# A decoder layer on one core: GpSimd's elementwise work in the mixer handed to VectorE, ScalarE and transposed rows

## The chip, the core and the metric

The kernel runs on one core of a Trainium2 chip. Its time is the device time of one execution in microseconds (us). The core has a matrix engine (TensorE, PE in the profile), a vector engine (VectorE, DVE), a scalar engine (ScalarE, ACT), a general engine (GpSimd, POOL) and a fifth one that here only starts transfers (SyncE, SP). Each engine takes its own queue in order and meets the others at semaphores.

## What is computed

One step of a decoder layer for two groups, a prompt of 1024 rows and 8 samples of one row, all of width 1024 in float32. First a mixer, then a gated feed-forward network; each is modulated by a condition and followed by a gated residual with a layer norm. The mixer has one input projection of 2816 columns, then two kinds of heads side by side, and one output projection:

```python
q, k, v, rq, rk, rv, rg = project_in(h, w_in)
...
rq = rope(rq.reshape(B, L, RET_HEADS, RET_DK), pos, RET_DK, RET_THETA)
rk = rope(rk.reshape(B, L, RET_HEADS, RET_DK), pos, RET_DK, RET_THETA) * (RET_DK ** -0.5)
...
def retention_output(o, g, gn_w):
    mu = jnp.mean(o, -1, keepdims=True)
    var = jnp.mean(jnp.square(o - mu), -1, keepdims=True)
    n = ((o - mu) * lax.rsqrt(var + GN_EPS)).reshape(o.shape[0], o.shape[1], RET_WIDTH)
    n = n * gn_w.astype(jnp.float32)
    return (jax.nn.silu(g.astype(jnp.float32)) * n).astype(g.dtype)
```

Attention (8 heads of 64, window 128) isn't touched by the change. Retention (4 heads of 128) rotates queries and keys, works over the prompt in 8 chunks of 128 rows with a state that decays by a constant of each head, and for each sample applies one step to a state of 4 heads x 128 x 128 that is read, updated and written back. Its output is normed per head, multiplied by the norm weight gn_w (one value for each of 512 columns) and by the gate silu(rg).

## The kernel before

Every large product is made of three matmuls (mm3, L215 to L217): each factor is split into a high part and a residual (wh and wl for weights, hT or mh and ml for rows), so each weight block needs a cast on ScalarE (wh, L269) and a subtraction on VectorE (wl, L281) before PE can use it. These blocks stream in by SyncE's queue (raw).

The prompt goes through the mixer in two halves of 512 rows. In order of time: a start with the modulation and the first projection (to about 66 us), the input projection of half 0 (to about 212), that of half 1 with attention and retention of half 0 and the samples beside it (to about 432), the output projection with the retention chunks of half 1 (pout, to about 565), then the feed-forward network. A small planner (Merge) takes pieces of work from several Python generators, by costs that these yield, and so fixes the order in the program; a tile scheduler then sets each engine's queue from it. So an edit that adds an instruction also shifts others in the queues.

The functions that matter:

- ropefull rotates 512 columns: a product with the cosines into its output (GpSimd), two half products with the sines into a temporary, and the sum (VectorE). It is called twice for each chunk (rr) and twice for the samples (rrs).
- ret_prep does both rotations of a chunk, scales its values by the decay (vg from zkv, GpSimd) and calls gate_prep, which makes the gate in the other half of vg and multiplies it by half of the norm weight, gnwh (GpSimd).
- ret_O and gnorm make the normed and gated rows sm of a chunk. ret_M transposes them by head on PE (bank rmt) and splits them into pages mh and ml, which the output projection takes. These pages belong to a half and not to a chunk.
- samp_ret loads the states st in four pages, scales them by gam (GpSimd), adds the new outer products (VectorE, 32 pieces) and writes them back. Its queries and keys are transposed in the bank srt from rrs.
- out_samp sums the four row groups of the samples' output projection (poutz) by samp_sum in a temporary from tmp512, a ring of three buffers shared with ropefull (rtmp) and with the evictions of pout (otmp, out_evac L1112 and L1113).

GpSimd also does the power in the norms (grs, lrs) and starts some transfers.

Of the kernel before, what the change touches and what calls it, by code (L numbers as in the profile page):

```python
# [13 lines left out]
ALU = mybir.AluOpType  # L14
# [163 lines left out]
def emit(ctx, tc, I, O):  # L178
# [133 lines left out]
    sinkb = small("sinkb", [128, 8])  # L312
    nsink = small("nsink", [128, 8])
    sink64 = small("sink64", [128, 2])
    gnwh = small("gnwh", [128, 512])
    ffs = hTs
    identr = small("identr", [128, 128], 1, F32R)

# [391 lines left out]
    def ropefull(out, x, cos, sin, rows):  # L710
        xv = x.rearrange("p (h s d) -> p h s d", h=4, s=2)
        ov = out.rearrange("p (h s d) -> p h s d", h=4, s=2)
        tmp = tmp512("rtmp")
        tv = tmp[0:rows].rearrange("p (h s d) -> p h s d", h=4, s=2)
        sb = sin.unsqueeze(1).to_broadcast([rows, 4, 64])
        G.tensor_tensor(out=ov, in0=xv, in1=cos.unsqueeze(1).unsqueeze(1).to_broadcast([rows, 4, 2, 64]), op=ALU.mult)
        V.scalar_tensor_tensor(out=tv[:, :, 0], in0=xv[:, :, 1], scalar=-1.0, in1=sb, op0=ALU.mult, op1=ALU.mult)
        V.tensor_tensor(out=tv[:, :, 1], in0=xv[:, :, 0], in1=sb, op=ALU.mult)
        V.tensor_tensor(out=out, in0=out, in1=tmp[0:rows], op=ALU.add)
# [7 lines left out]
    def gate_prep(dst, rg, rows):  # L727
        A.activation(out=dst, in_=rg, func=AF.Tanh, scale=0.5)
        yield 0, 1000
        V.scalar_tensor_tensor(out=dst, in0=dst, scalar=1.0, in1=rg, op0=ALU.add, op1=ALU.mult)  # L730
        G.tensor_tensor(out=dst, in0=dst, in1=gnwh[0:rows], op=ALU.mult)

    def gnorm(o, n_out, gate, rows, scaled, pe, dve):
        st = small("gst", [128, 4, 6], 2)
# [21 lines left out]
    def ret_prep(c):  # L756
        rr = page(f"rr{c}")
        vg = page(f"vg{c}")
        tab = tab_box[0]
        cos, sin = tab[:, c * 64:(c + 1) * 64], tab[:, 512 + c * 64:576 + c * 64]  # L760
        ropefull(rr[:, 0:512], zqg[c][:, 0:512], cos, sin, 128)
        yield 0, 1000, 1300
        ropefull(rr[:, 512:1024], zkv[c][:, 0:512], cos, sin, 128)
        G.tensor_tensor(out=h4(vg[:, 0:512]), in0=h4(zkv[c][:, 512:1024]), in1=bc4(C("vsc"), 128), op=ALU.mult)
        yield 0, 1000, 1300
        yield from gate_prep(vg[:, 512:1024], zqg[c][:, 512:1024], 128)
        R[c] = {"rr": rr, "vg": vg}
        zkv.pop(c)
        zqg.pop(c)
# [52 lines left out]
    def ret_M(c):  # L822
        sm = R.pop(c)["sm"]
        b = bank("rmt")
        for h in range(4):
            PE.transpose(b[:, h * 128:(h + 1) * 128], sm[:, 512 + h * 128:640 + h * 128], ident)
        half, tl = c // 4, c % 4
        for j in range(2):
            mh, ml = mix_pages(half, 2 + j)
            src = b[:, j * 256:(j + 1) * 256].rearrange("p (a c) -> p a c", a=2)  # L830
            oh = mh[:, 0:1024].rearrange("p (a c) -> p a c", a=2)[:, :, tl * 128:(tl + 1) * 128]
            ol = ml[:, 0:1024].rearrange("p (a c) -> p a c", a=2)[:, :, tl * 128:(tl + 1) * 128]
            A.copy(out=oh, in_=src)
            V.tensor_sub(out=ol, in0=src, in1=f(oh))

    def ret_chunk(c):
        yield "need", ("in", c // 4, "rg")
# [107 lines left out]
    def samp_ret():  # L945
        yield "need", ("zs", "rv")
        zkvs, zqgs = zs["r"][32:40], zs["r"][0:8]
        vd = drp.tile([8, 512], F32, name="vd")
        G.dma_start(out=vd, in_=zkvs[:, 512:1024])
        yield "need", ("zs", "rq")  # L950
        state_pg = []
        for i in range(4):
            t = page(f"st{i}")
            SP.dma_start(out=t[:, 0:1024].rearrange("p (a e) -> p a e", a=8),
                         in_=I["state"][8 * i:8 * i + 8].rearrange("a d e -> d a e"))
            state_pg.append(t)
        rr = page("rrs")
        ropefull(rr[0:8, 0:512], zqgs[:, 0:512], C("src")[0:8], C("srs")[0:8], 8)
        ropefull(rr[0:8, 512:1024], zkvs[:, 0:512], C("src")[32:40], C("srs")[32:40], 8)
        vb = []  # L960
        for i in range(4):
            t = page(f"vb{i}")
            SP.dma_start(out=t[:, 0:1024], in_=vd[2 * i:2 * i + 2, :].rearrange("(o b) e -> o (b e)", o=1)
                         .to_broadcast([128, 1024]))
            vb.append(t)
        yield 0, 4000, 3000
        b = bank("srt")
        for i in range(8):
            PE.transpose(b[:, i * 8:(i + 1) * 8], rr[0:8, i * 128:(i + 1) * 128], ident[0:8, 0:8])
        qs = small("qss", [128, 32])  # L970
        ks = small("kss", [128, 32])
        V.tensor_copy(out=qs.rearrange("p (b h) -> p h b", b=8), in_=b[:, 0:32].rearrange("p (h b) -> p h b", h=4))
        V.tensor_scalar(ks.rearrange("p (b h) -> p h b", b=8), b[:, 32:64].rearrange("p (h b) -> p h b", h=4),
                        128.0 ** -0.5, None, op0=ALU.mult)
        yield 200, 800
        qm = page("qm")[:, 0:256]
        G.memset(qm, 0.0)
        qm4 = qm.rearrange("p (b h r) -> p b h r", b=8, h=4)
        for s in range(8):
            V.tensor_copy(out=qm4[:, s, :, s], in_=qs[:, 4 * s:4 * s + 4])  # L980
        bo = bank("sro")
        for i in range(4):
            st = state_pg[i]
            G.tensor_tensor(out=st[:, 0:1024].rearrange("p (b h e) -> p b h e", b=2, h=4),
                            in0=st[:, 0:1024].rearrange("p (b h e) -> p b h e", b=2, h=4),
                            in1=C("gam").unsqueeze(1).unsqueeze(3).to_broadcast([128, 2, 4, 128]), op=ALU.mult)
            for j in range(8):
                bh = 8 * i + j
                sl = slice(j * 128, (j + 1) * 128)
                V.scalar_tensor_tensor(out=st[:, sl], in0=vb[i][:, sl], scalar=ks[:, bh:bh + 1], in1=st[:, sl],  # L990
                                       op0=ALU.mult, op1=ALU.add)
            yield 0, 4500, 2200
            for j in range(8):
                bh, h = 8 * i + j, j % 4
                PE.matmul(bo[32 * h:32 * h + 8, 0:128], lhsT=qm[:, bh * 8:bh * 8 + 8], rhs=st[:, j * 128:(j + 1) * 128],
                          start=i == 0 and j < 4, stop=i == 3 and j >= 4)
            SP.dma_start(out=O["nrs"][8 * i:8 * i + 8].rearrange("a d e -> d a e"),
                        in_=st[:, 0:1024].rearrange("p (a e) -> p a e", a=8))
            yield 430, 0
        yield "need", ("zs", "rg")  # L1000
        gt = page("gts")
        yield from gate_prep(gt[0:8, 0:512], zqgs[:, 512:1024], 8)
        yield 0, 1500
        so = tmp512("so")
        for h in range(4):
            A.copy(out=so[0:8, h * 128:(h + 1) * 128], in_=bo[32 * h:32 * h + 8, 0:128])
        yield from gnorm(so[0:8, :], gt[0:8, 512:1024], gt[0:8, 0:512], 8, False, 0, 1300)
        yield 0, 1200
        b = bank("smt")
        for h in range(4):  # L1010
            PE.transpose(b[:, h * 8:(h + 1) * 8], gt[0:8, 512 + h * 128:640 + h * 128], ident[0:8, 0:8])
        V.tensor_copy(out=mixTs[:, 4:8, 0:8], in_=b[:, 0:32].rearrange("p (h b) -> p h b", h=4))
        done.add("mixs_r")
        yield 100, 0

# [98 lines left out]

    def out_samp(cg, psz):
        cs = slice(cg * 512, (cg + 1) * 512)
        tmp = tmp512("otmp")
        samp_sum(tmp[0:8], psz, 512)
        V.tensor_tensor(out=tmp[0:8], in0=tmp[0:8], in1=gates[1, "s"][0:8, cs], op=ALU.mult)
        x = xrs[0]  # L1120
        V.scalar_tensor_tensor(out=x[0:8, cs], in0=x[0:8, cs], scalar=ALPHA, in1=tmp[0:8], op0=ALU.mult, op1=ALU.add)
# [648 lines left out]
    def misc_loads():  # L1770
        tc.keep_in_program_order(SP.dma_start(out=sinkb, in_=I["sinks"].to_broadcast([128, 8])))
        tc.keep_in_program_order(SP.dma_start(out=sink64[0:64, 0:1], in_=I["sinks64"]))
        tc.keep_in_program_order(SP.dma_start(out=gnwh, in_=I["gn_w"].to_broadcast([128, 512])))
        G.tensor_scalar(nsink, sinkb, -1.0, None, op0=ALU.mult)
        G.tensor_scalar(sink64[0:64, 1:2], sink64[0:64, 0:1], -1.0, None, op0=ALU.mult)
        G.tensor_scalar(gnwh, gnwh, 0.5, None, op0=ALU.mult)
        t = page("tab")
        SP.dma_start(out=t[:, 0:1024], in_=I["tab"])
        tab_box.append(t)
# [84 lines left out]
```

## Time and profile before

| | |
|---|---|
| runs | 1281.33, 1281.74, 1282.64 us; median 1281.74 |
| profiled execution | 1281.65 us, its span 1279.8 us |
| mean granted clock of TensorE | 0.975 |
| busy: TensorE, VectorE, ScalarE, GpSimd | 1218.8, 883.8, 449.3, 152.6 us |
| GpSimd's product with the cosines, L716 | 16 of 128x512, 1368 and 1443 ns each; 2 of 8x512, 1164 ns |
| GpSimd's product with the norm weight, L731 | 8 of 128x512, 1724 ns each; 1 of 8x512, 2336 ns |
| GpSimd's scaling of the values, L764 | 8 of 128x512, 1112 ns each |
| GpSimd's scaling of the states, L984 | 4 of 128x1024, 2074 ns each |

A row of a list of waits reads: engine, tile and line that waited, then the engine, tile and line that released it, then the sum in us, the number of waits and the longest. A row of a timeline reads: start, duration, engine, line, operation, tiles and shapes, and in brackets the engine's idle time just before with its releaser. A row of windows reads: stretch and its length, then for each engine its busy time and in brackets its instructions, then the granted clock (PEclk, 1.00 is full), the share of the transfer engines and GB/s. A row of groups ends in busy us, mean ns of one, and the idle time ahead.

### The profile page before, as it was taken

How to read it: one execution, taken by the hardware profiler on the slowest of the kernel's cores; microseconds unless marked ns; L12 is line 12 of the kernel's file. 1: busy time of each engine (PE TensorE's matmuls, PEld its weight loads, DVE VectorE, ACT ScalarE, POOL GpSimd, SP SyncE). 2: the span in 40 equal slices, each digit the busy share in tenths (PEclk: the TensorE clock that was granted, in tenths of full speed). 3: DMA queues.
4: the chain of work that ended last, by engine and by line, in shares of the span. 5: the costliest groups of instructions: out<-in, count | busy, mean ns of one | idle time of the engine just before them, and what ended most of it. 6: DMA issues, size and time to landing. Idle time of an engine off the chain costs nothing.

```text
span 1279.8 us, 20189 instructions
## 1 busy us (share of the span) xinstructions
PE 1218.8 (95%) x7922; PEld 1026.1 (80%) x7922; DVE 883.8 (69%) x1712; ACT 449.3 (35%) x812; POOL 152.6 (12%) x170
## 2 busy tenths in 40 slices
PE   8999979999999989797999999999999999999996
PEld 5877756778777758576999999999999987888885
DVE  2456665787655587696777766767676759849697
ACT  2335523344553223536323222322233234534420
POOL 0000031321002231110101110111101110000011
PEclk8999989899999989989999999999999999999999
DMA  9732477152225332502334443543354399846631
GB/s 284 238 112 67 134 243 266 50 172 80 67 66 205 126 103 71 198 33 87 119 119 167 145 160 108 178 150 135 121 169 157 124 338 398 276 154 212 201 126 66
DMA packets 144136, 199.07 MB, mean 156 GB/s; under 512 B 8140, under 2 KB 85172, under 8 KB 144025
## 3 DMA queue, kind: packets, MB, share of 16 engines
q1 hardware_dynamic: 133512, 161.37, 39.3%
q0 software_dynamic: 10528, 36.42, 7.5%
q8 instruction: 62, 1.02, 0.3%
q14 instruction: 34, 0.27, 0.1%
HBM read 155.02 MB, written 43.77 MB: 155 GB/s over the span
## 4 chain that ended last, share of the span: by engine, by line
PE 36%; issue 34%; DVE 8%; POOL 5%; DMA 2%; ACT 1%; POOLq 0%; DVEq 0%; SPq 0%; ACTq 0%
PE dn L216 4%; PE dn L217 4%; PE dn L215 4%; PE pin L215 4%; PE pin L216 3%; PE pin L217 3%; PE pout L216 2%; POOL fd L1485 1%; PE pout L217 1%; PE pout L215 1%; POOL fs L1489 1%; POOL ws L1518 1%; PE adab L874 1%; DVE z L1595 1%; DMA z<-yd 1%
## 5 line engine op out<-in xcount | busy, mean ns | idle before, releaser
L215 PE MATMUL pin<-wh,hT 128*128 128x512 f32 (+1 forms) x320 | 129.6, 409 | 0.1
L216 PE MATMUL pin<-wl,hT 128*128 128x512 f32 (+1 forms) x320 | 125.6, 393 | 3.8 <-DVE wl L281 3.8
L217 PE MATMUL pin<-wh,hT 128*128 128x512 f32 (+1 forms) x320 | 125.0, 392 | 0.4 <-DVE hT L340 0.4
L215 PE MATMUL up<-hb,wa_h 128*128 128x256 f32 (+1 forms) x352 | 100.2, 285 | 2.0 <-ACT hb L1300 1.5
L216 PE MATMUL up<-hb,wa_h 128*128 128x256 f32 (+1 forms) x352 | 100.0, 284 | 0.7 <-DVE hb L1301 0.7
L217 PE MATMUL up<-hb,wa_l 128*128 128x256 f32 (+1 forms) x352 | 99.6, 283 | 0.4 <-DVE wa_l L1347 0.4
L215 PEld LDWEIGHTS pin<-wh,hT 128*128 128x128 f32 x320 | 61.0, 191 | 26.5 <-issue 13.5
L281 DVE TENSOR_TENSOR wl<-raw,wh 128x1024 fp32r<-128x1024 f32 (+1 forms) x62 | 74.0, 1195 | 7.1 <-PE ptp L657 3.5
L217 PEld LDWEIGHTS pin<-wh,hT 128*128 128x128 f32 x320 | 61.6, 193 | 16.1 <-issue 2.2
L216 PEld LDWEIGHTS pin<-wl,hT 128*128 128x128 f32 x320 | 62.0, 194 | 14.5 <-DVE wl L281 4.3
L1452 ACT ACTIVATE sg<-sg 128x256 f32<-128x256 f32 (+1 forms) x66 | 27.7, 420 | 120.9 <-DVE sg L1451 120.9
L215 PEld LDWEIGHTS up<-hb,wa_h 128*128 128x128 f32 x352 | 66.9, 190 | 2.9 <-ACT hb L1300 1.9
L216 PEld LDWEIGHTS up<-hb,wa_h 128*128 128x128 f32 x352 | 67.0, 190 | 1.3 <-DVE hb L1301 1.3
L217 PEld LDWEIGHTS up<-hb,wa_l 128*128 128x128 f32 x352 | 66.6, 189 | 0.7 <-DVE wa_l L1347 0.7
L269 ACT CAST wh<-raw 128x1024 fp32r<-128x1024 f32 (+1 forms) x62 | 62.8, 1022 | 11.4 <-DMA raw<-in_w_in 6.6
L216 PE MATMUL pout<-wl,mh 128*128 128x512 f32 x128 | 53.0, 415 | 13.6 <-DVE wl L281 13.6
L1457 DVE TENSOR_TENSOR uc<-up,tp 128x256 f32<-128x256 f32 x66 | 28.2, 427 | 39.0 <-PE up L217 38.9
L1451 DVE TENSOR_TENSOR sg<-up,tp 128x256 f32<-128x256 f32 (+1 forms) x66 | 27.9, 423 | 38.2 <-PE up L217 38.2
L1485 POOL DMA_DIRECT2D fd<-sg x33 | 19.8, 599 | 280.2 <-DVE sg L1458 280.2
L1471 ACT COPY hTs<-sg 128x8 f32<-128x8 f32 x22 | 4.3, 198 | 138.8 <-DVE sg L1458 138.8
L215 PE MATMUL pout<-wh,mh 128*128 128x512 f32 x128 | 52.8, 418 | 0.0
L217 PE MATMUL pout<-wh,ml 128*128 128x512 f32 x128 | 52.2, 409 | 0.0
(502 smaller groups left out, 3695.9 us busy)
## 6 DMA issues: line engine op xcount, KB each, us to landing
wr<-in_w_up SPq DMA_DIRECT2D x44, 512.0 KB, 5.4
raw<-in_w_in SPq DMA_DIRECT2D x38, 512.0 KB, 4.0
adr<-in_w_ada_ffn SPq DMA_DIRECT2D x24, 512.0 KB, 3.9
wd<-in_w_down SPq DMA_DIRECT2D x22, 512.0 KB, 5.1
dr<-fs SPq DMA_DIRECT2D x44, 256.0 KB, 3.6
dr<-ws SPq DMA_DIRECT2D x44, 256.0 KB, 3.0
fd<-sg POOLq DMA_DIRECT2D x33, 256.0 KB, 4.0
dr<-fd SPq DMA_DIRECT2D x33, 256.0 KB, 8.2
```

What stands on the lines that cost most here:

```text
L215: PE.matmul(ps, lhsT=ah, rhs=bh, start=start, stop=False, skip_group_check=onto)
L216: PE.matmul(ps, lhsT=ah, rhs=bl, start=False, stop=False, skip_group_check=onto)
L217: PE.matmul(ps, lhsT=al, rhs=bh, start=False, stop=stop, skip_group_check=onto)
L269: A.copy(out=h[:, 0:n], in_=src[:, 0:n])
L281: V.tensor_sub(out=l[:, 0:n], in0=src[:, 0:n], in1=f(h[:, 0:n]))
L874: PE.matmul(b[32 * q:32 * q + 32, :], lhsT=cT[:, k2 * 4 + q, :], rhs=rr[q // 2][:, (q % 2) * 512:(q % 2) * 512 + 512], start=k2 == 0, stop ...
L1451: V.tensor_tensor(out=dst, in0=ps, in1=add, op=ALU.add)
L1452: A.activation(out=dst, in_=dst, func=AF.Silu)
L1457: V.tensor_tensor(out=t, in0=ps, in1=add, op=ALU.add)
L1485: G.dma_start(out=two(d) if p == 4 else d, in_=ap)
L1489: G.dma_start(out=d.rearrange("a p c -> p a c"), in_=t[:, 0:1024].rearrange("p (a c) -> p a c", a=2))
L1518: G.dma_start(out=d.rearrange("a p c -> p a c"), in_=t[:, 0:1024].rearrange("p (a c) -> p a c", a=2))
```

## The change

The cosine product of every rotation goes from GpSimd to VectorE. The scaling of the values becomes four multiplies of 128x128 on ScalarE, that of a state page four of 128x2x128 on ScalarE. The norm weight no longer goes into the gate. It is loaded as four rows, transposed on PE and halved into gnT, one column for each head, and is put on when the transposed rows are split in ret_M: mh is the product on ScalarE, ml the same product less mh on VectorE, in pieces of one head (four and four for a chunk, where two copies and two subtractions of two heads each stood). For the samples it is put on in the copy after their transpose. out_samp gets a tile of its own (otz) in place of one of the ring.

```diff
@@ ropefull
-        G.tensor_tensor(out=ov, in0=xv, in1=cos.unsqueeze(1).unsqueeze(1).to_broadcast([rows, 4, 2, 64]), op=ALU.mult)
+        V.tensor_tensor(out=ov, in0=xv, in1=cos.unsqueeze(1).unsqueeze(1).to_broadcast([rows, 4, 2, 64]), op=ALU.mult)
@@ gate_prep
         V.scalar_tensor_tensor(out=dst, in0=dst, scalar=1.0, in1=rg, op0=ALU.add, op1=ALU.mult)
-        G.tensor_tensor(out=dst, in0=dst, in1=gnwh[0:rows], op=ALU.mult)
@@ ret_prep
-        G.tensor_tensor(out=h4(vg[:, 0:512]), in0=h4(zkv[c][:, 512:1024]), in1=bc4(C("vsc"), 128), op=ALU.mult)
+        for h in range(4):
+            sl = slice(h * 128, (h + 1) * 128)
+            A.mul(vg[:, sl], zkv[c][:, 512 + h * 128:640 + h * 128], C("vsc")[:, h:h + 1])
@@ ret_M
-            src = b[:, j * 256:(j + 1) * 256].rearrange("p (a c) -> p a c", a=2)
...
-            A.copy(out=oh, in_=src)
-            V.tensor_sub(out=ol, in0=src, in1=f(oh))
+            for a in range(2):
+                h = 2 * j + a
+                src, g = b[:, h * 128:(h + 1) * 128], gnT[:, h:h + 1]
+                A.mul(oh[:, a], src, g)
+                V.scalar_tensor_tensor(out=ol[:, a], in0=src, scalar=g, in1=f(oh[:, a]), op0=ALU.mult,
+                                       op1=ALU.subtract)
@@ samp_ret
-            G.tensor_tensor(out=st[:, 0:1024].rearrange("p (b h e) -> p b h e", b=2, h=4),
-                            in0=st[:, 0:1024].rearrange("p (b h e) -> p b h e", b=2, h=4),
-                            in1=C("gam").unsqueeze(1).unsqueeze(3).to_broadcast([128, 2, 4, 128]), op=ALU.mult)
+            s4 = st[:, 0:1024].rearrange("p (b h e) -> p b h e", b=2, h=4)
+            for h in range(4):
+                A.mul(s4[:, :, h], s4[:, :, h], C("gam")[:, h:h + 1])
...
-        V.tensor_copy(out=mixTs[:, 4:8, 0:8], in_=b[:, 0:32].rearrange("p (h b) -> p h b", h=4))
+        V.tensor_tensor(out=mixTs[:, 4:8, 0:8], in0=b[:, 0:32].rearrange("p (h b) -> p h b", h=4),
+                        in1=gnT.unsqueeze(2).to_broadcast([128, 4, 8]), op=ALU.mult)
@@ out_samp
-        tmp = tmp512("otmp")
+        tmp = small("otz", [128, 512])
@@ misc_loads
-        tc.keep_in_program_order(SP.dma_start(out=gnwh, in_=I["gn_w"].to_broadcast([128, 512])))
+        gr = page("gnr")
+        SP.dma_start(out=gr[0:4, 0:128], in_=I["gn_w"].rearrange("o (h p) -> (o h) p", p=128))
+        b = bank("gnt")
+        PE.transpose(b[:, 0:4], gr[0:4, 0:128], ident[0:4, 0:4])
+        V.tensor_scalar(gnT, b[:, 0:4], 0.5, None, op0=ALU.mult)
...
-        G.tensor_scalar(gnwh, gnwh, 0.5, None, op0=ALU.mult)
```

How this moves the queues is shown at two places. In the changed program the lines of gnorm are one lower and those after ret_prep one to five higher, and the numbers behind the names differ.

ScalarE's queue at the start of the output projection, before: the normed rows sm5 of a second chunk, the four copies of two chunks into mh (of half 1, banks rmt of two numbers), and the weight cast that follows.

```order
L751 ACTIVATE sm5_4102<-ro_4163,gnm_4177,grs_4176 128x128 x4
L833 CAST mh1_2_4235<-rmt_4230 128x2x128
L833 CAST mh1_3_4239<-rmt_4230 128x2x128
L833 CAST mh1_2_4235<-rmt_4278 128x2x128
L833 CAST mh1_3_4239<-rmt_4278 128x2x128
L269 CAST wh50_4264<-raw50_4188 128x1024
```

The same place after:

```order
L750 ACTIVATE sm5_4144<-ro_4205,gnm_4219,grs_4218 128x128 x4
L836 ACTIVATE mh1_2_4277<-rmt_4272,gnT_77 128x128 x2
L836 ACTIVATE mh1_3_4283<-rmt_4272,gnT_77 128x128 x2
L836 ACTIVATE mh1_2_4277<-rmt_4327,gnT_77 128x128 x2
L836 ACTIVATE mh1_3_4283<-rmt_4327,gnT_77 128x128 x2
L269 CAST wh50_4310<-raw50_4230 128x1024
L765 ACTIVATE vg6_4290<-zkv6_3015,cst_66 128x128 x4
L728 ACTIVATE vg6_4290<-zqg6_3683 128x512
```

Eight pieces of mh now stand ahead of the same weight cast (wh50 in both), and the scaling of the values follows it.

VectorE's queue there, before, from the last piece of ml to the subtraction wl of that weight block, with evictions of the first output tiles (pout) between:

```order
L834 TENSOR_TENSOR ml1_3_4240<-rmt_4278,mh1_3_4239 128x2x128
L899 TENSOR_SCALAR gates_4209<-gsels_4301 9x512
L1112 TENSOR_TENSOR otmp_4329<-pout0_3958,gate1_4049 128x512
L1113 SCALAR_TENSOR_TENSOR xr0_0_4254<-xr0_0_4254,otmp_4329 128x512
L1112 TENSOR_TENSOR otmp_4332<-pout1_3959,gate1_4049 128x512
L1212 BN_STATS lst_4627<-xr0_0_4254 128x6
L1113 SCALAR_TENSOR_TENSOR xr0_1_4256<-xr0_1_4256,otmp_4332 128x512
L281 TENSOR_TENSOR wl50_4304<-raw50_4188,wh50_4264 128x1024
```

And after:

```order
L837 SCALAR_TENSOR_TENSOR ml1_2_4278<-rmt_4327,gnT_77,mh1_2_4277 128x128
L903 TENSOR_SCALAR gates_4251<-gsels_4354 9x512
L837 SCALAR_TENSOR_TENSOR ml1_3_4284<-rmt_4327,gnT_77,mh1_3_4283 128x128
L717 SCALAR_TENSOR_TENSOR rtmp_4363<-zkv7_3017,tab_707 128x4x64
L718 TENSOR_TENSOR rtmp_4363<-zkv7_3017,tab_707 128x4x64
L837 SCALAR_TENSOR_TENSOR ml1_3_4284<-rmt_4327,gnT_77,mh1_3_4283 128x128
L1117 TENSOR_TENSOR otmp_4384<-pout0_3996,gate1_4091 128x512
L1118 SCALAR_TENSOR_TENSOR xr0_0_4300<-xr0_0_4300,otmp_4384 128x512
L1117 TENSOR_TENSOR otmp_4387<-pout1_3997,gate1_4091 128x512
L716 TENSOR_TENSOR rr7_4344<-zqg7_3685,tab_707 128x512
L281 TENSOR_TENSOR wl50_4357<-raw50_4230,wh50_4310 128x1024
```

The pieces of ml are spread over more rows, a cosine product (L716) stands ahead of wl, and a statistics row and one eviction row (L1212 and the second L1113) have gone behind it.

More of the change, by code (lines that the diff above doesn't have):

```diff
@@ L314, in emit @@
     sink64 = small("sink64", [128, 2])
-    gnwh = small("gnwh", [128, 512])
+    gnT = small("gnT", [128, 4])
     ffs = hTs
```

## The prediction

> **What bounds the kernel now.** I read the page's first part, then TensorE's list of waits, then the timelines of the waiting stretches, then windows over them for the clock.
>
> ```profile
> PE 1218.8 (95%) x7922; PEld 1026.1 (80%) x7922; DVE 883.8 (69%) x1712; ACT 449.3 (35%) x812; POOL 152.6 (12%) x170
> ...
> PE pout L216 <- DVE wl L281: 13.6, 3, 7.6
> PE rmt L826 <- DVE sm L754: 4.9, 2, 3.4
> PE srt L969 <- DVE rrs L719: 4.2, 2, 2.3
> PE pin L216 <- DVE wl L281: 3.8, 2, 3.2
> ...
> PE spt L1081 <- DVE Ps L1077: 2.1, 1, 2.1
> ```
>
> TensorE (PE) is busy for 95% of the span, and the change adds one transpose to its 7922 matmuls. So a gain can only come out of PE's waits, or out of time that it spends at half clock. The five rows hold 28.6 us, all in the mixer, and in each VectorE (DVE) releases PE. They lie at six places, named A to F here. A has three waits; E, not shown, is the second of the rmt row, 1.5 us at 497.5:
>
> ```profile
> 180.64 0.41 PE L969 MATMUL srt<-cst,rrs 8*128 8x8 f32 x4 [2.27 <-DVE rrs L719]
> 182.94 0.59 PE L969 MATMUL srt<-cst,rrs 8*128 8x8 f32 x4 [1.90 <-DVE rrs L719]
> 186.77 0.80 PE L216 MATMUL pin<-wl,hT 128*128 128x512 f32 x1 [3.24 <-DVE wl L281]
> ...
> 258.75 0.63 PE L826 MATMUL rmt<-cst,sm 128*128 128x128 f32 x4 [3.39 <-DVE sm L754]
> ...
> 412.26 0.24 PE L1081 MATMUL spt<-cst,Ps 64*128 64x64 f32 x1 [2.11 <-DVE Ps L1077]
> ...
> 470.73 0.80 PE L216 MATMUL pout<-wl,mh 128*128 128x512 f32 x1 [5.55 <-DVE wl L281]
> ...
> 545.06 0.80 PE L216 MATMUL pout<-wl,mh 128*128 128x512 f32 x1 [7.58 <-DVE wl L281]
> ```
>
> Why DVE is late at A to D is read from its timeline beside GpSimd's (POOL's). The reader is to compare durations of one shape; the two ACT rows are weight casts, for later:
>
> ```profile
> 173.35 0.41 DVE L717 SCALAR_TENSOR_TENSOR rtmp<-zsr,cst 8x256 f32<-8x256 f32 x1
> ...
> 178.31 4.58 DVE L719 TENSOR_TENSOR rrs<-rrs,rtmp 8x512 f32<-8x512 f32 x2
> ...
> 183.91 1.67 DVE L990 SCALAR_TENSOR_TENSOR st<-vb,kss,st 128x128 f32<-128x128 f32 x6
> ...
> 252.87 1.51 DVE L717 SCALAR_TENSOR_TENSOR rtmp<-zqg,tab 128x256 f32<-128x256 f32 x1
> ...
> 409.83 1.22 DVE L1075 TENSOR_TENSOR mxs<-mxs 64x1 f32<-64x1 f32 x1
> ...
> 456.49 0.68 DVE L754 TENSOR_TENSOR sm<-sm,vg 128x512 f32<-128x512 f32 x1
> ...
> 462.50 5.05 DVE L1113 SCALAR_TENSOR_TENSOR xr<-xr,otmp 128x512 f32<-128x512 f32 x1
> ...
> 468.86 0.68 DVE L1113 SCALAR_TENSOR_TENSOR xr<-xr,otmp 128x512 f32<-128x512 f32 x1
> 469.45 1.22 DVE L281 TENSOR_TENSOR wl<-raw,wh 128x1024 fp32r<-128x1024 f32 x1
> ...
> 462.48 1.06 POOL L764 TENSOR_TENSOR vg<-zkv,cst 128x512 f32<-128x512 f32 x1
> ...
> 465.95 1.04 POOL L764 TENSOR_TENSOR vg<-zkv,cst 128x512 f32<-128x512 f32 x1
> ...
> 171.07 1.05 ACT L269 CAST wh<-raw 128x1024 fp32r<-128x1024 f32 x1
> ...
> 462.21 1.04 ACT L269 CAST wh<-raw 128x1024 fp32r<-128x1024 f32 x1
> ```
>
> L1113 takes 0.68 us alone, and 5.05 us while POOL runs four elementwise operations back to back (the two shown and two L716 between, 462.48 to 466.99). L717 goes from 0.41 to 1.51 for the same elements per partition, a pair of L719 from some 1.4 (0.706 each, below) to 4.58, and a row of one element, L1075, takes 1.22. Over the mixer this excess, over the time of the same shape alone, adds up to some 20 us of DVE time, an estimate of mine.
>
> [...]
>
> The other price of a wait is the clock:
>
> ```profile
> core 0: us, PE busy (x) PEld busy (x) DVE busy (x) ACT busy (x) POOL busy (x), PEclk, DMA share, GB/s
> 178.70:182.10 3.40, 0.41 (x4) 0.32 (x4) 3.40 (x2) 0.00 (x0) 3.40 (x2) 1.00 0.83 319
> 182.10:192.40 10.30, 6.22 (x17) 4.96 (x18) 9.58 (x36) 0.00 (x0) 0.50 (x2) 0.50 0.54 162
> 214.00:330.00 116.00, 111.74 (x697) 88.86 (x688) 91.06 (x218) 49.04 (x104) 24.85 (x21) 0.97 0.34 103
> 253.80:257.20 3.40, 1.56 (x7) 0.94 (x5) 3.40 (x4) 0.08 (x1) 2.92 (x3) 1.00 0.00 0
> 414.20:421.10 6.90, 6.90 (x31) 5.11 (x30) 3.13 (x11) 1.46 (x3) 0.00 (x0) 0.51 0.26 78
> ...
> 468.80:475.70 6.90, 4.97 (x12) 3.91 (x13) 6.90 (x12) 0.00 (x0) 1.67 (x1) 0.51 0.15 58
> ```
>
> After the waits of A, C and D the granted clock is 0.5 for 7 to 10 us (after F too). Half of PE's busy time there is lost: 3.1 us at A, 3.4 at C, 2.5 at D. After B (1.56 us busy in a stretch of 3.40) it stays full.
>
> **The change, part by part.**
>
> ```profile
> L719 DVE TENSOR_TENSOR rr<-rr,rtmp 128x512 f32<-128x512 f32 x16 | 11.0, 706 | 0.0
> ...
> L834 DVE TENSOR_TENSOR ml<-rmt,mh 128x256 fp32r<-128x256 f32 x16 | 6.7, 419 | 2.1 <-ACT mh L833 1.9
> ...
> L990 DVE SCALAR_TENSOR_TENSOR st<-vb,kss,st 128x128 f32<-128x128 f32 x32 | 8.7, 341 | 0.0
> ...
> L751 ACT ACTIVATE sm<-ro,gnm,grs 128x128 f32<-128x128 f32 x32 | 12.2, 458 | 31.8 <-DVE gnm L748 31.8
> ...
> L833 ACT CAST mh<-rmt 128x256 fp32r<-128x256 f32 x16 | 6.0, 378 | 13.1 <-PE rmt L826 8.2 <-DVE ml L834 4.9
> ```
>
> *Work added.* DVE gets 16 cosine multiplies of 128x512 and two of 8x512. The nearest row is L719, 11.0 us for 16, so 12.4 us for 18; the 32 pieces of the residual in ret_M, by L990's 8.7 us for 32, replace L834's 6.7: 2.0 more. Together DVE gains 14.4 us and loses the 20 us of excess; the row is about balanced, but what it gets is spread over eight chunks, and what it loses sits in front of PE's waits. ScalarE (ACT) gets 32 decay pieces (12.2 us by L751), 16 state pieces of 128x2x128 (6.0 by L833), and 32 pieces for 16 in ret_M (12.2 less 6.0): 24 us on an engine busy for 35%. POOL keeps its small powers and its DMAs. The norm weight's transpose costs PE some 0.1 us at the start; its rows land long before.
>
> *A, samples, gain 6.0.* Without POOL's state scaling beside it, the rotation of the two 8x512 rows is, from 173.35 on, four L717/L718 (0.33 apart), two L716 and two L719 (0.6 each): ready at 177.1, before PE comes at 178.4. Both srt waits go. The state pieces on ACT (6.0 us behind the weight cast that ends at 172.1) are done near 178. Then DVE goes through six L990 (1.67) from 179.6 on and wl (1.22): PE, done with srt at 179.4, gets wl at 182.4 and waits 3.0 instead of 7.4. That is 4.4 us. The 3.1 us of half clock I halve, since I can't tell which side of 0.41 and 1.56 us busy the stretch falls: 1.6. Bounds: 2 if the state pieces hold up L990, 10 if no wait is left.
>
> *B, retention chunk 0, gain 2.2.* Three L717/L718 lose 1.1, 1.1 and 0.9 us, and the group norm's small row ahead of them about 1.1. Against that stand two more multiplies of 0.6 in the same queue, and rather less PE work placed between this norm and its transpose. I take 1.2 us of the 3.39 as left; bounds 0 and 3.4.
>
> *C, sample softmax, gain 3.1.* Three rows of a 64-row chain lie under POOL's rotations there and lose some 2.5 us, more than the 2.11 that PE waits. Of the 3.4 us at half clock I take 1.0; tiny matmuls stay in that stretch. Bounds 2.1 and 5.5.
>
> *D, output projection, gain 6.9.* From the second norm's product (456.49, about 0.9 earlier without the excess ahead of it) DVE now has, up to wl: that product, eight pieces of ml, three L716, two L719, L717, L718, the gate row, two L1117 and one L1118, some 9 us, with no 5.05 in it. The eight pieces of mh and ml alternate between ACT and DVE (each mh piece waits for the last ml piece); a round is 0.38 + 0.27 us, and DVE's rows between them are counted already. The weight cast wh behind the eight on ACT then ends at about 463.0, as it does now (463.25), and wl at some 466.0. PE has three more matmuls ahead and comes at 465.3. The wait falls from 5.55 to 0.7; 2.0 of the 2.5 us of clock go with it. Bounds: 8, and 0 if a round takes 1.5 us. Besides, the 0.4 us that the first row's 13.6 hold beyond 7.58 and 5.55, a wl at 454.79 under POOL, go.
>
> *E and F.* At E PE has one more matmul ahead of its wait: 0.2. F changes nothing for good: no POOL operation runs there, DVE is behind by its own work.
>
> ```profile
> 532.56 1.23 DVE L1347 TENSOR_TENSOR hs_1l<-ts,hs_1h 128x1024 fp32r<-128x1024 f32 x1 [1.11 <-ACT hs_1h L1346]
> ...
> 543.81 1.19 DVE L281 TENSOR_TENSOR wl<-raw,wh 128x1024 fp32r<-128x1024 f32 x1
> ```
>
> The own tile for sample sums lets its copy on ACT run early, but on DVE three L408 and the gate product now all stand ahead of this wl, where one L408 stood: 1.8 us more, of which the 1.11 us of idle time ahead of hs_1l take up most. F loses 0.4. As F hangs on DVE's chain from PE's end of the first output group (503.6), gains made before it carry through.
>
> *Sum.* 0.5 (the shorter pin wait: pieces of rotation no longer stand ahead of that wl) + 6.0 + 2.2 + 3.1 + 6.9 + 0.4 + 0.2 - 0.4 - 0.1 = 18.8. Against it I set 2.0 for one new wait of B's size: in 214 to 330 DVE is busy for 91.06 of 116 us and gets its rows in new places. The profiled execution of 1281.65 (span 1279.8; the median 1281.74 is the same) becomes 1264.9.
>
> [...]
>
> **Rivals.** *More goes:* the half clocks of A, C and D vanish wholly and B's wait too: 1.5 + 2.4 + 0.5 of clock, 1.2 at B, 0.7 at D, and nothing new, 2.0, make 8.3 more: 1256.6. For it: B's stretch shows that 46% busy holds the clock. Against: A keeps a wait of 3 us.
>
> *D is not won:* the wait re-forms as F's is, by queue length. If a round of the alternation takes 1.5 us, wh ends near 470 and D gives nothing: 1272. For it: eight muls ahead of wh where four stood. Against: L833 waited 4.9 us for ml in 16 pieces, 0.3 each.
>
> [...]
>
> *Slower:* the alternation in ret_M becomes the bound. 32 more rounds than before; where a wl (1.22) or an L716 stands in DVE's queue between two of them, ACT waits 1.2 us, and with it the casts behind: 38 us in all, 1303 if all of it reached PE. It decides from 0.5 us per round on the path, 16.8 over 32. L833's 0.3 each speaks against it.
>
> **Chances.** Forecast 0.55 (1259 to 1270), more goes 0.17, D not won 0.13, no difference 0.06, slower 0.09. The range leaves out the slower case, most of no difference, and the far tails of the others: 1254 to 1277. Faster 0.85, same 0.06, slower 0.09.
>
> **What would show it.** Right: no L719 on rrs over 0.75 us, no srt wait, L1113 at 0.68 throughout; waits of about 3 at A, 1 at B, none at C, under 1 at D, 1.3 at E and 8 at F; clock 0.5 still after F, not after D. Wrong: D's wait over 3 us with ACT's mh pieces each waiting for ml; new waits of pin on wl between 214 and 330; F much shorter, which would say that the sample tile's ring did hold DVE back.

## The result and the profile after

| | median (lowest to highest) | before, same chip | ratio, 95% interval |
|---|---|---|---|
| changed kernel, 4 runs | 1267.85 us (1267.69 to 1269.28) | 1281.53 | 0.9897 (0.988 to 0.9914) |
| the same kernel in a later series, 4 runs | 1263.81 us (1262.48 to 1265.36) | 1281.49 | 0.9862 (0.9848 to 0.9877) |

The change makes the kernel about 1.0 to 1.4% faster. The prediction was 1264.9 (1254 to 1277). The two series of one program lie 4.0 us apart, more than their intervals allow for; what differs between the two profiled executions is shown below, at places A and B. Profiled executions: 1269.28 us (span 1267.3, granted clock 0.977) and 1265.36 us (span 1263.5, 0.981). Each is the slowest of its four.

TensorE's waits in the profile after, as one line of busy times and four rows of the list:

```profile
PE 1219.0 (96%) x7923; PEld 1024.9 (81%) x7923; DVE 874.9 (69%) x1747; ACT 470.8 (37%) x876; POOL 94.7 (7%) x130
...
PE pout L216 <- DVE wl L281: 9.8, 2, 8.6
PE pin L216 <- DVE wl L281: 3.3, 1, 3.3
...
PE rmt L827 <- DVE sm L753: 1.7, 2, 1.3
PE pin L215 <- ACT qk L781: 1.6, 1, 1.6
```

The rows srt, of 4.2 us, and spt, of 2.1, are gone. The five rows of before held 28.6 us; these four hold 16.4, one of them (qk, 1.6) new. PE's own busy time is what it was. DVE is busy for 8.9 us less, although it has 35 instructions more: by these figures the stretching under POOL was worth more than the rows that it took over.

The places A, B, B's new wait, D and F on PE's timeline:

```profile
182.69 0.79 PE L216 MATMUL pin<-wl,hT 128*128 128x512 f32 x1 [3.31 <-DVE wl L281]
...
252.00 0.63 PE L827 MATMUL rmt<-cst,sm 128*128 128x128 f32 x4 [0.41 <-DVE sm L753]
...
255.13 0.39 PE L215 MATMUL pin<-wh,hT 128*128 128x256 f32 x1 [1.63 <-ACT qk L781]
...
457.98 0.50 PE L216 MATMUL pout<-wl,mh 128*128 128x512 f32 x1 [1.23 <-DVE wl L281]
...
530.71 0.80 PE L216 MATMUL pout<-wl,mh 128*128 128x512 f32 x1 [8.56 <-DVE wl L281]
```

A's three waits (7.4) are one of 3.31, C is gone, D is 1.23 for 5.55, and F is longer than before, 8.56 for 7.58. DVE and ACT behind these rows:

```profile
176.72 1.28 DVE L719 TENSOR_TENSOR rrs<-rrs,rtmp 8x512 f32<-8x512 f32 x2
...
179.84 1.67 DVE L994 SCALAR_TENSOR_TENSOR st<-vb,kss,st 128x128 f32<-128x128 f32 x6
...
454.70 0.69 DVE L1118 SCALAR_TENSOR_TENSOR xr<-xr,otmp 128x512 f32<-128x512 f32 x1
...
253.45 0.37 ACT L836 ACTIVATE mh<-rmt,gnT 128x128 fp32r<-128x128 f32 x1 [0.42 <-DVE ml L837]
254.24 0.37 ACT L836 ACTIVATE mh<-rmt,gnT 128x128 fp32r<-128x128 f32 x1 [0.42 <-DVE ml L837]
254.51 0.58 ACT L781 COPY qk<-rtp 128x512 f32<-128x512 f32 x1
```

The pair L719 on rrs takes 1.28 us where it took 4.58, and the residual row at D 0.69 where it took 5.05. The last three rows are the alternation: each mh piece waits 0.42 us for the ml piece before it, so a round is 0.79 us (253.45 to 254.24), and the copy qk that PE needs stands behind it.

The clock, by windows of the profile after and then of the second series:

```profile
177.80:181.20 3.40, 1.58 (x13) 1.03 (x11) 1.87 (x9) 2.06 (x4) 0.21 (x1) 1.00 1.02 383
181.20:188.10 6.90, 5.41 (x13) 4.25 (x14) 6.90 (x29) 0.00 (x0) 0.00 (x0) 0.51 0.84 264
...
252.90:256.30 3.40, 1.76 (x17) 1.31 (x19) 2.45 (x7) 2.56 (x9) 0.00 (x0) 1.00 0.94 305
...
256.30:259.70 3.40, 3.40 (x15) 1.74 (x16) 2.62 (x6) 3.40 (x7) 0.00 (x0) 0.50 0.20 20
...
409.90:413.30 3.40, 3.40 (x12) 0.99 (x11) 3.35 (x10) 1.72 (x4) 0.00 (x0) 0.50 0.03 12
...
455.00:480.00 25.00, 23.49 (x144) 20.10 (x143) 22.40 (x49) 9.93 (x21) 3.60 (x3) 1.00 0.36 117
```

```profile
181.60:185.10 3.50, 3.50 (x10) 2.68 (x10) 3.50 (x14) 0.00 (x0) 0.00 (x0) 0.51 0.63 189
...
256.30:259.70 3.40, 3.40 (x32) 3.30 (x29) 3.15 (x7) 3.27 (x6) 0.00 (x0) 1.00 0.50 154
```

Half clock stays at A, appears at B's new wait and is gone at D. The second series has the same waits (3.31 at A, 8.57 at F) and yet half the half clock at A and none at B: which stretch is granted at half rate differs between these two executions. By the windows above that is 2.7 us of PE's work at A against 1.75, and 1.7 at B against none, 2.7 of the 3.8 us between the two spans.

Where the gain came from, by the start of the same matmul in the two traces (before less after, each stretch for itself): A +4.6, B +0.9, C +3.4, D +6.0, E +0.7, F -0.7, start of the feed-forward network -1.7, the rest -0.2, and -0.4 ahead of A: 12.5 us, the difference of the spans (1279.8 less 1267.3).

### The profile page after: what moved, and what is told of

Its sections match the earlier page's. It is cut to its first block, busy times and chain, and to the rows that moved or that the text cites. A ratio compares the mean times of both kernels' runs of the same rounds, so it can differ in the third digit from the quotient of the medians.

```text
span 1267.3 us, 20192 instructions
## 1 busy us (share of the span) xinstructions
PE 1219.0 (96%) x7923; PEld 1024.9 (81%) x7923; DVE 874.9 (69%) x1747; ACT 470.8 (37%) x876; POOL 94.7 (7%) x130
## 4 chain that ended last, share of the span: by engine, by line
PE 44%; issue 29%; DVE 7%; POOL 4%; DMA 1%; ACT 0%; POOLq 0%; SPq 0%; DVEq 0%
PE dn L216 4%; PE dn L215 4%; PE dn L217 4%; PE pin L215 4%; PE pin L216 4%; PE pin L217 4%; PE up L215 2%; PE up L217 2%; PE up L216 2%; PE pout L215 2%; PE pout L216 2%; PE pout L217 2%; PE adab L878 1%; POOL fd L1490 1%; DVE z L1600 1%
## 5 line engine op out<-in xcount | busy, mean ns | idle before, releaser
L216 PEld LDWEIGHTS pin<-wl,hT 128*128 128x128 f32 x320 | 61.9, 193 | 14.4 <-DVE wl L281 3.4
L216 PE MATMUL up<-hc,wc_h 128*128 128x256 f32 (+1 forms) x176 | 50.1, 285 | 0.0
```

The source lines that it names most:

```text
L216: PE.matmul(ps, lhsT=ah, rhs=bl, start=False, stop=False, skip_group_check=onto)
```

## The experiments

Four kernels below rest on the changed kernel with the sums of the samples back in the ring (u_otz), the others on the kernel named.

**The own tile for sample sums.** On the changed kernel:

```diff
-        tmp = small("otz", [128, 512])
+        tmp = tmp512("otmp")
```

> The whole change, but the samples' sums in the output projection take their temporary from the ring of three again. My working: DVE's own rows set the wait F, so 1267 to 1268, the same as with the own tile or 0.4 us faster. Rival: the ring held DVE back, then F grows by 2 to 5 us and the time is 1270 to 1273.

Measured: 1264.88 us (1260.69 to 1266.72), ratio 0.9861 (0.9842 to 0.988). F's wait is 7.58 us, as before the change, for 8.56 with the own tile:

```profile
528.80 0.80 PE L216 MATMUL pout<-wl,mh 128*128 128x512 f32 x1 [7.58 <-DVE wl L281]
```

Against the first series of the changed kernel that is 3 us faster, which I first took for the price of the own tile. So both were run again, unchanged:

> The changed kernel itself, beside u_otz on the same chip. If the own tile for sample sums costs what the two profiles say (0.98 us of the wait F and one stretch of half clock, 1.7), it is 2 to 3 us slower than u_otz; if that was chance, they differ by less than 1.

> u_otz once more, beside the changed kernel on the same chip: 2 to 3 us faster than it if the own tile has a price, else within 1.

Measured: 1263.81 and 1265.0 us (ratio of u_otz_b 0.9864, 0.9847 to 0.9881). The own tile costs PE 1 us of wait at F, in every profile, and no time that can be measured; the 3 us were the spread of one program. From here on u_otz stands for the changed kernel.

**GpSimd's rows back, into a tile that nobody reads.** This leaves PE's, DVE's and ACT's queues as they are. On u_otz, 26 GpSimd rows with two operands:

```diff
@@ ropefull
+        junk = small("junk", [128, 512])
+        G.tensor_tensor(out=junk[0:rows].rearrange("p (h s d) -> p h s d", h=4, s=2), in0=xv,
+                        in1=cos.unsqueeze(1).unsqueeze(1).to_broadcast([rows, 4, 2, 64]), op=ALU.mult)
@@ ret_prep
+        G.tensor_tensor(out=h4(small("junk", [128, 512])[:, 0:512]), in0=h4(zkv[c][:, 512:1024]), in1=bc4(C("vsc"), 128), op=ALU.mult)
```

> As u_otz, but GpSimd also does the 18 cosine products and the 8 scalings of the values once more, into a scratch tile that nobody reads. The queues of PE, DVE and ACT hold the same rows in the same order as in u_otz, so only GpSimd is busier. [...] Queue theory (the gain came from rows in other places and from products that are ready sooner): at most 1 to 2 us slower, for the norms' powers that now wait on GpSimd.

Measured: 1282.21 us, ratio 1.0004 (0.9994 to 1.0014), 11 runs. That is 17.3 us more than u_otz, whose gain in the same series was 16.8, and far more than the 1 to 2 of the queue theory. At A, the timelines of DVE, POOL and PE:

```profile
184.99 7.55 DVE L998 SCALAR_TENSOR_TENSOR st<-vb,kss,st 128x128 f32<-128x128 f32 x6
...
184.87 1.27 POOL L718 TENSOR_TENSOR junk<-zqg,tab 128x512 f32<-128x512 f32 x1
...
191.35 1.04 POOL L769 TENSOR_TENSOR junk<-zkv,cst 128x512 f32<-128x512 f32 x1
...
182.27 0.41 PE L977 MATMUL srt<-cst,rrs 8*128 8x8 f32 x4 [4.13 <-DVE rrs L722]
...
193.73 0.79 PE L216 MATMUL pin<-wl,hT 128*128 128x512 f32 x1 [9.20 <-DVE wl L281]
```

and the window over it:

```profile
182.60:199.60 17.00, 6.54 (x20) 5.11 (x19) 16.21 (x36) 0.00 (x0) 9.50 (x9) 0.50 0.35 105
```

Six DVE rows that took 1.67 us take 7.55 while six POOL rows run back to back (the first and the last are shown). The wl behind them is then late by as much, PE waits 9.20 us for 3.31, and 17 us pass at a granted clock of 0.50. No data passes from these rows to any other, so it is their running that costs. Nor is it GpSimd's queue: the memset that stands behind the rows ends at 192.6, ahead of all that needs it.

But the rows do not come back where they ran before the change. They wait for their inputs alone, so they run in two trains, 14 rows from 173 to 192 us and 12 from 385 to 402. By the start of the same matmuls, PE falls 12.8 us behind u_otz at the first train and 4.6 at the second, where four DVE rows of the attention take 4.93 us for 1.14:

```profile
397.71 4.93 DVE L647 TENSOR_SCALAR P<-P,den 128x256 f32<-128x256 f32 x4
```

At B, C, D and E no extra row runs, and PE's waits there are u_otz's. So the run shows that GpSimd's rows alone, with the other queues unchanged, cost DVE (7.55 us for 1.67) and PE (12.8 and 4.6 us) this much. It says nothing of B to E, and that the loss is as large as the whole gain is chance.

**The same rows with one operand.** As above, with `G.tensor_scalar(junk, x, -1.0, None, op0=ALU.mult)` in both places.

> As u_otz, with GpSimd's 26 extra rows reading one operand in place of two (a multiply by a constant into the scratch tile). [...]

Measured: 1276.49 us, ratio 0.9966 (0.9954 to 0.9978). That is 11.6 us more than u_otz, two thirds of the loss above; against the kernel before in its own series it gains 4.35 us of u_otz's 16.8. But it loses them in another way, as the timelines of DVE, POOL and PE at A show:

```profile
178.72 2.05 DVE L997 SCALAR_TENSOR_TENSOR st<-vb,kss,st 128x128 f32<-128x128 f32 x6
180.69 1.21 DVE L281 TENSOR_TENSOR wl<-raw,wh 128x1024 fp32r<-128x1024 f32 x1
181.83 5.69 DVE L997 SCALAR_TENSOR_TENSOR st<-vb,kss,st 128x128 f32<-128x128 f32 x16
...
180.80 2.46 POOL L718 TENSOR_SCALAR junk<-zqg 128x512 f32<-128x512 f32 x1
...
196.05 0.31 POOL L984 MEMSET qm<- 128x256 f32 x1
...
196.71 1.04 PE L1002 MATMUL sro<-st,qm 128*8 128x128 f32 x16 [7.98 <-DVE qm L987]
```

The six DVE rows take 2.05 us for 1.67 and the sixteen behind wl 5.69, where the same sixteen take 4.29 with no POOL row beside them (in the run of the states alone, below): a third at most is added, where two operands made it more than fourfold (7.55 for 1.67). The POOL row that starts 0.1 us after wl takes 2.46 us where its kind take 1.49 to 1.65 otherwise. What costs most is POOL's queue: a memset of a sample tile stands behind the whole train, until 196.05, and PE waits 7.98 us for it. So the run tells the two causes apart at A, and does not give a clean price for stretching over the whole kernel.

**Each part alone, on the kernel before.** Only the cosine products on DVE (G becomes V in ropefull); only the state scaling on ACT; only the value scaling on ACT; only the norm weight on transposed rows (with ret_M's eight pieces). The edits are those of the change's diff.

> The kernel before with the cosine products alone moved to DVE; value and state scaling and the norm weight stay on GpSimd. [...] If DVE's added 12 us are what counts: no change or slower.

> The kernel before with the state scaling alone moved to ScalarE; rotations, value scaling and norm weight stay on GpSimd. My working of A put its whole gain down to this piece: the pair of L719 on rrs falls from 4.58 to 1.4 us, the srt waits shrink to 0 to 2 us, 3 to 6 us faster (1276 to 1279). Rival, after the run with the rotations alone, whose srt waits were gone although the states stayed on GpSimd: the rotations' own products on GpSimd were the cause, then the srt waits stay and the time is 1280 to 1282.

> The kernel before with the value scaling alone moved to ScalarE. [...] Rival: the four pieces on ScalarE delay weight casts: 1 to 3 us slower.

> The kernel before with the norm weight alone moved to the transposed rows (64 pieces in ret_M in place of 32, no product with the norm weight on GpSimd). My working: little lies on GpSimd's products with the norm weight beside PE's waits: 0 to 3 us faster (1279 to 1282). Rival, the alternation of ScalarE and DVE over the pages mh and ml: 2 to 10 us slower, with waits of pout on wl behind the eight pieces.

| part alone | us | ratio, 95% interval | srt (4.2) | spt (2.1) | D (5.55) |
|---|---|---|---|---|---|
| cosine products | 1269.8 | 0.9902 (0.9886 to 0.9918) | 0 | 0.2 | 1.8, and 1.1 for otmp |
| states | 1275.55 | 0.9964 (0.9951 to 0.9977) | 0 | 2.4 | 5.5 |
| values | 1276.01 | 0.9958 (0.9946 to 0.997) | 4.2 | 0.7 | 3.6 |
| norm weight | 1278.66 | 0.9983 (0.9968 to 0.9997) | 3.9 | 0.9 | 1.8, and 3.4 for otmp |

From the lists of waits of the cosine part and of the norm weight:

```profile
PE pout L216 <- DVE wl L281: 9.4, 2, 7.6
...
PE pout L215 <- DVE otmp L1112: 1.1, 1, 1.1
...
PE spt L1081 <- DVE Ps L1077: 0.2, 1, 0.2
```

```profile
PE pout L216 <- DVE wl L281: 9.9, 3, 7.6
PE srt L971 <- DVE rrs L719: 3.9, 2, 2.2
PE pout L215 <- DVE otmp L1115: 3.4, 1, 3.4
...
PE spt L1084 <- DVE Ps L1080: 0.9, 1, 0.9
```

The sums of pout on wl hold D beside F's 7.6, which no part moves; where no srt row stands, there is no such wait. The parts give 11.9, 5.3, 4.8 and 3.0 us in the table's order (below 1281.67 for the first and the last, 1280.84 for the two between), 25 together against 14 to 18 for the whole: they remove the same waits. The states alone remove srt, and so do the cosine products alone; spt and D are cut by three of the four. The cosine products alone give 11.9 us, most of what the whole gives, where no gain was to come if DVE's added work were what counts; the values gain 4.8 us, where ScalarE's four pieces were to cost 1 to 3.

Two of these runs also test the stretching itself. With the states alone, PE's and DVE's queues hold the same rows in the same order as before through the whole mixer, and the pair L719 on rrs takes 1.28 us for 4.58. With the values alone, PE's queue is the same too, and so is DVE's around B, C and D; at D two of the four POOL rows are gone. DVE, POOL and PE there:

```profile
458.83 3.09 DVE L1115 SCALAR_TENSOR_TENSOR xr<-xr,otmp 128x512 f32<-128x512 f32 x1
...
458.81 1.31 POOL L716 TENSOR_TENSOR rr<-zqg,tab 128x512 f32<-128x512 f32 x1
460.07 1.29 POOL L716 TENSOR_TENSOR rr<-zkv,tab 128x512 f32<-128x512 f32 x1
...
465.10 0.58 PE L216 MATMUL pout<-wl,mh 128*128 128x512 f32 x1 [3.59 <-DVE wl L281]
```

The residual row takes 3.09 us for 5.05 and again ends only after the last POOL row; PE waits 3.59 for 5.55. At B one POOL row less takes the third L717 from 1.26 to 0.41 and the wait from 3.39 to 2.52, and at C POOL is done before L1075 (here L1077), which goes from 1.22 to 0.14 us, and the wait from 2.11 to 0.68. So at all four places fewer POOL rows shorten DVE's rows and PE's wait with the order of PE's and DVE's rows unchanged.

**F, by more weight blocks in hand.** On u_otz, in the second output projection `depth[:] = [3, 2, 1]` becomes `[4, 3, 3]`, so that more wl rows are made ahead; then the first block of the feed-forward network is also given priority (`tc.high_priority(offset=40 if i == 0 else 0)` around its split and sums).

> u_otz with the look-ahead of the second output projection one to two blocks deeper (its list 3, 2, 1 becomes 4, 3, 3), which puts the awaited wl ahead of the layer norm's rows on DVE. If DVE's order is what makes the wait F (7.6 us and some 3 us of half clock), a part of it goes: 2 to 8 us faster than u_otz (1257 to 1263). If the wait moves to the next block or loads come late, no change (1264 to 1266).

> i_u433 with the first feed-forward weight block's cast and sums put ahead of the last norm's rows on ScalarE and DVE. In i_u433 the wait F was gone and PE waited 4.7 us for that cast instead, which stood behind a row that waited for DVE. If the order on ScalarE holds it, 3 to 8 us faster than u_otz (1257 to 1262); if the norm's own chain bounds the change of stage, no difference (1263 to 1266).

Measured: 1264.05 us (ratio 0.9857, 0.9839 to 0.9874) and 1262.28 (0.9849, 0.9834 to 0.9864). PE's waits in the first of the two, and ACT's timeline at 546 us:

```profile
PE up L215 <- ACT wa_h L1351: 4.7, 1, 4.7
...
PE pout L216 <- DVE wl L281: 1.8, 2, 1.2
```

```profile
546.29 1.24 ACT L1238 ACTIVATE xr<-xr,lrs 128x1024 f32<-128x1024 f32 x1 [9.22 <-DVE lrs L1236]
547.43 1.03 ACT L1351 CAST wa_h<-wr 128x1024 fp32r<-128x1024 f32 x1
```

F's 7.6 us are gone from pout, and PE waits 4.7 for the first feed-forward weights instead, whose cast stands on ACT behind a row that waits 9.22 us for the layer norm. With priority this wait is 4.0, for another row of ACT. In these two runs F's wait moves on to the next work rather than away, and that stands behind the layer norm's chain. The two kernels are not told from u_otz by their intervals.

**The alternation.** On the changed kernel ret_M makes the four mh pieces first and the four ml pieces after:

```diff
+        parts = []
...
+                parts.append((b[:, h * 128:(h + 1) * 128], gnT[:, h:h + 1], oh[:, a], ol[:, a]))
+        for src, g, oh, ol in parts:
+            A.mul(oh, src, g)
+        for src, g, oh, ol in parts:
+            V.scalar_tensor_tensor(out=ol, in0=src, scalar=g, in1=f(oh), op0=ALU.mult, op1=ALU.subtract)
```

> The changed kernel with ret_M's pieces written in another order: the four multiplies of a chunk on ScalarE first, then the four rows on DVE, so that no piece of mh waits for ml. In the changed kernel's trace a round of the alternation takes 0.79 us, and at B three rounds stand ahead of a copy (qk) that PE waits 1.63 us for, with 1.7 us of half clock behind it. If the alternation is the price, that wait falls under 0.5 and D's 1.23 shrinks: 1 to 4 us faster than the changed kernel (which gave 1263.8 and 1267.9 in two series): 1260 to 1265. If ScalarE's number of pieces is what delays the copy, the wait stays near 1.2 and the time is the changed kernel's.

Measured: 1262.79 us (1261.7 to 1263.7), ratio 0.9855 (0.9838 to 0.9873); the same kernel without the edit, 1263.81. At B:

```profile
250.41 1.14 ACT L838 ACTIVATE mh<-rmt,gnT 128x128 fp32r<-128x128 f32 x4 [2.49 <-PE rmt L827]
251.42 0.60 ACT L781 COPY qk<-rtp 128x512 f32<-128x512 f32 x1
...
252.76 0.39 PE L215 MATMUL pin<-wh,hT 128*128 128x256 f32 x1 [1.52 <-DVE ml L840]
```

Four mh pieces take 1.14 us, and the copy qk starts 1.7 us after PE's transposes (249.74) and not 2.5 (254.51 after 252.00). PE waits nearly as long, 1.52 for 1.63, now for DVE's last ml piece, and D's wait is 1.83 for 1.23. So the alternation set which engine came last at B and hardly the length of the wait; it cost no time that can be measured. An order of ret_M that frees both engines earlier was not tried.

What else sets this wait is seen in the norm weight alone, which has eight pieces too. PE there:

```profile
259.05 1.06 PE L504 MATMUL pinz<-raw,hTs 128*32 128x512 f32 x8
260.52 0.39 PE L215 MATMUL pin<-wh,hT 128*128 128x256 f32 x1 [0.40 <-ACT qk L779]
```

Eight matmuls of the samples' projection (pinz) stand in the gap, as they do in the kernel before, and the wait is 0.40. In the changed kernel the new order has moved them to 247.58. With the cosine products alone they have moved as well (247.60), the pieces are still four, and the wait is 1.00.

## Why the prediction held, step by step

- **DVE rows stretched by GpSimd.** Shown at A from both sides: with the 26 rows added into scratch nothing else changed and the awaited DVE rows stretched (7.55 for 1.67), and with the states alone removed they shrank (1.28 for 4.58). At B, C and D it is shown by the values alone (3.09 for 5.05 at D). The case of no difference falls there: the order of the rows alone does not set these waits, since these runs keep it and the waits shrink (D's to 3.59). How one engine holds up the other is not shown by any run. How much of the rest of B's and D's gain the new order gave is not separated. The size of the stretching was put at 20 us: DVE got 12.3 us of cosine products and 4.4 more for ml (11.1 for 6.7, forecast 2.0), and is busy for 8.9 us less, so by these figures some 25 us of stretching went, an estimate.
- **A, forecast 0.5 + 6.0, measured 4.6.** The wait was forecast as 3.0 and is 3.31. The failing term is the clock: 1.6 of the 3.1 us were to be won, and in the first profile 2.7 are lost still, so 0.4 was won. My bracket of 0.41 us busy in 3.40 (half) and 1.56 (full) said nothing: 1.58 us of 3.40 at A was followed by half clock, and so was 1.76 at B. PE's busy time in the stretch ahead did not tell the grant at these places. Nor did the wait: in the second series it is the same 3.31 us, and 3.50 us are at half clock where 6.90 were. I also put this gain down to the state scaling. The states alone do remove srt, but so do the cosine products alone.
- **B, forecast 2.2, measured 0.9.** The old wait went further than forecast (0.41 for 1.2). The step that failed is that nothing new stands behind it: PE waits 1.63 us for qk, and half clock followed (3.40 us at 0.50, 1.7 us). Eight rows in place of four make qk later (alone they make the wait 0.40), and the new order took 1.06 us of PE's work out of the gap (with that and four rows it is 1.00). I had set 2.0 against the sum for "one new wait of B's size" without a place. This is that wait, and it costs 3.3 in the first profile and 1.6 in the second.
- **C, forecast 3.1, measured 3.4.** The wait is gone. 3.40 us at half clock stay where 6.90 were.
- **D, forecast 6.9 + 0.4, measured 6.0.** The wait is 1.23 (forecast 0.7) and full clock follows. The rival that D is not won, from 1.5 us per round, lost: a round is 0.79. I had 0.65 (0.38 + 0.27); what I put at 0.27 is an idle time of 0.42. One row was read wrongly: the weight cast that I held against D (462.21) belongs to the next block, and its own is the one two us earlier. The sum did not depend on it, as DVE's rows set the wait on both readings.
- **E, forecast 0.2, measured 0.7; F, forecast -0.4, measured -0.7.** F's wait grew by 0.98, not 0.4. It is the own tile's, since without it the wait is 7.58. That the earlier gains carry through F held: the group of F begins 14.4 us earlier (530.71 for 545.06).
- **After the mixer.** I forecast no change, and 1.7 us were lost at the start of the feed-forward network. There are three stretches of half clock there (577.20 to 580.60, 584.00 to 587.40 and 590.80 to 597.70) where before there were two. I did not test this; in the profile of the second series there are two again, and it differs here by about 1 us, so the larger part is where half clock happened to fall.
- **The rival "slower".** It needed 0.5 us per round on the path. A round was 0.79, but hardly on the path: r_four takes the rounds away and gains 1 us, within noise.

The sum of 16.8 stands against 13.7 us in the first series and 17.7 in the second. With a program whose own series lie 4 us apart, this sum cannot be tested more finely than that. That it comes within 1 us of the second is in part luck: the terms add up to 18.8, and the same stretches give 12.5 in the first profile. A, B and D are 4.5 us of what is missing and the start of the feed-forward network 1.7, and the 2.0 set against the sum covers a third of it.

## What to carry to other kernels

Look for one instruction shape whose duration differs by a factor on the same engine (here 0.68 and 5.05 us), and for what runs on GpSimd at those moments. Rows that GpSimd did "for free" were paid here by VectorE: six of its rows took 7.55 us for 1.67 beside rows with two operands, and 2.05 beside rows with one. Price such a row by what VectorE waits in front of the engine that bounds the kernel, not by the share of busy time. A part removed alone may win the same wait as another part, so the gains of parts are not added. When rows are put back as a test, look where they run: they may not run where they did. Before a few microseconds are explained, run the same kernel twice.

## What the runs showed of the hardware

Not expected was how far the stretching goes. Beside a train of GpSimd rows with two operands VectorE ended about one row per POOL row at A (six rows in 7.55 us, 1.26 each, under six POOL rows of 1.04 to 1.27), and not even that at D: one row took 5.05 us under four POOL rows, and 3.09 where only two ran. Rows of VectorE with one tensor and one column of scalars were stretched as well (L647, 4.93 us for 1.14). With one operand the same train cost VectorE 0.4 us over six rows (2.05 for 1.67) and 1.4 over sixteen (5.69 for 4.29), and a GpSimd row that started 0.1 us after wl took 2.46 us for some 1.5. Beside these rows VectorE's six took 0.34 us each, and not the 1.5 of a POOL row. So at A what GpSimd's rows cost VectorE went with their operands: 5.88 us over these six rows with two, 0.38 with one.

Also not expected was that half clock comes and goes with the same waits: 6.90 us at A in one execution and 3.50 in another, with 3.31 us of wait in both. At A and B this is 2.7 of the 3.8 us between the two profiled executions. That it is also what sets the medians of the two series apart is not shown; the mean granted clock of every run fits it, 0.977 to 0.979 in the first and 0.981 to 0.984 in the second.
